# Fixing ScalarE's order in the output projections of a two-layer trunk

## The chip, the cores and the metric

The kernel runs on one core of a Trainium2 chip. The metric is the device time of one execution in microseconds (us); the median over some executions counts. The core has a matrix engine (TensorE, PE in the profile), a vector engine (VectorE, DVE), an engine for activation functions and copies (ScalarE, ACT), GpSimd (POOL, unused here) and SyncE (SP), which issues the DMAs. Each engine works through its own queue in order; semaphores make one wait for another.

## The reference

Two layers of a transformer-like trunk over 3 blocks of 128 tokens (one block of context, two of a sample), 1024 features each. Every layer has a mixer (retention and windowed attention in layer 0, differential attention and Fourier mixing in layer 1), whose concatenated output goes through an output projection, and then a gated FFN with 2816 hidden features. What matters here, for one layer:

```python
out = concat([...], -1) @ w_out                          # output projection, 1024 -> 1024
x = layer_norm(ALPHA * x + g1 * out, ln_g[l, 0], ln_b[l, 0])
u = layer_norm(x) * (1.0 + sc2) + sh2                    # input of the FFN
ffn = (silu(u @ w_gate) * (u @ w_up)) @ w_down
x = layer_norm(ALPHA * x + g2 * ffn, ln_g[l, 1], ln_b[l, 1])
```

All tensors are float32; `sh2`, `sc2`, `g1`, `g2` come from a conditioning vector by `w_mod`.

## The kernel before

A float32 product is made of three passes of a faster matmul type: each operand is split into a rounded part (`r`, a cast on ScalarE) and the rest (`l`, a subtraction on VectorE), and r·r, l·r and r·l are added in PSUM (`in_block`, L372). Weights arrive by DMA into 5 raw buffers and are split by `split` (L172): `S.copy` at L173, `V.tensor_tensor` at L175. A split weight sits in one of 5 pairs of buffers (`wr`, `wl`).

The change is in `w_out_phase` (L435), which runs once in each layer, between the mixer and the FFN. It has these steps, for the blocks b = 0, 1, 2:

- P (`project`): the output projection of a block, in two halves of 512 columns with 24 matmuls each (tiles `wo`), then residual and sums on VectorE (tile `so`), and the first square of the layer norm on ScalarE (L298).
- A and B (`norm`): the rest of the first layer norm (VectorE L366, then a square on ScalarE), and then the second layer norm's scaling into `so` (L313, on ScalarE; for block 2 L311, on VectorE). Each of the two needs a chain of eight small VectorE instructions (L189 to L201, and L309 at the end of the second), an inverse square root.
- F (`to_u`, by way of `make_u` and `make_u_half`): eight row transposes of `so` on TensorE (tiles `puo`), eight scalings by `sc2` and `sh2` (tiles `ufo`, L330, ScalarE; half of block 2's on VectorE, L327), two casts to the rounded part `urf` (L333, ScalarE) and two subtractions to the rest `ulf` (L334, VectorE).
- G and U: load and split the first 256 columns of the gate and the up matrix, in two units each (`r_gh`, `l_gh`, `r_uh`, `l_uh`).
- H (`head`): 24 matmuls of the first gate columns (tile `hg`), a Silu (tile `hsg`, L484, ScalarE), 24 matmuls of the first up columns (tile `hu`) and the product (L487, VectorE); the transposes of this product (tile `ht`) follow in the next head. `hg` and `hu` take turns in two PSUM banks, so that the next head's `hg` needs the bank which the Silu reads.
- X (`hold_splits`): from here on, VectorE's half of each weight split and of each scaling in `mod_steps` has to come after block 2's last `ulf` on VectorE. (`gated`, L169). M is empty in both layers.

`WORDER` (L38) lists the steps for each layer. Its order is the order of priority, not the order in the queues: a planner goes over all instructions with its own model of their durations, and each engine's queue takes the instruction that is ready in that model and stands first in the source; transposes and some matmuls have their priority raised (`boost`). `tc.issue_after(ins)` adds an edge without a wait: the instructions of its block that run on the engine of `ins` are queued behind `ins`. Instructions of the FFN and of `mod_steps` (the conditioning for later, tiles `mraw` and `z`: a DMA, a scaling on ScalarE at L247, additions on VectorE at L250) can move into this phase where the model sees an engine idle.

Of the kernel before, what the change touches and what calls it, by code (L numbers as in the profile page):

```python
# [14 lines left out]
AF = mybir.ActivationFunctionType  # L15
# [4 lines left out]
P = 128  # L20
# [5 lines left out]
NFP = D_FF // 256  # L26
HOLD = 4
RHOLD = (3, 5)
WMODS = ((), ())
TMODS = ()  # L30
SMODS = (((0, 5), (1, 1), (1, 0), (1, 3), (1, 4), (1, 2)), ((1, 5),))
NLNW = 8
# [2 lines left out]
NFILL = 2  # L35
NBUSY = 12
LOADS = (("m", 0, 1), ("kv", 0), ("m", 1, 1), ("q", 0), ("m", 2, 2), ("q", 2), ("m", 4, 2), ("kv", 4), ("q", 4), ("m", 6, 2), ("q", 6))
WORDER = ("P0 P1 G A0 B0 F0 A1 B1 P2 U H0 F1 A2 B2 F2 X H1 M H2", "G P0 P1 A0 B0 A1 B1 U P2 F0 F1 H0 A2 B2 F2 X H1 M H2")  # L38
CORDER = "V0 V1 N0 V2 C N1 N2"
DORDER = "D0 A0 D1 B0 A1 F0 U B1 D2 T A2 F1 B2 F2 K"  # L40
NWR = 5
# [23 lines left out]
def trunk_kernel(ctx: ExitStack, tc: tile.TileContext, a: dict):  # L65
    nc = tc.nc
    mm = nc.tensor.matmul
    V, S, G, SY = nc.vector, nc.scalar, nc.gpsimd, nc.sync
# [47 lines left out]
    def boost(f, *args, **kw):  # L116
        with tc.high_priority(offset=BOOST):
            return f(*args, **kw)  # L118
# [24 lines left out]
    ones = ones_all[:, 0:32]  # L143
# [20 lines left out]
        SY.dma_start(t, src)  # L164
        return t

    gate = [None]

    def gated():  # L169
        return tc.issue_after(gate[0].ins) if gate[0] is not None else nullcontext()  # L170

    def split(t, r, lo):  # L172
        S.copy(r, t)  # L173
        with gated():
            V.tensor_tensor(lo, t, r, ALU.subtract)  # L175
        return r, lo

    def split_unit(src, shape, name, rl=None):
        t = raw_unit(src, shape, f"raw_{name}")
        if rl is None:  # L180
            rl = (perm.tile([P] + shape, F32R, tag="wr", name=f"r_{name}", bufs=NWR),
                  perm.tile([P] + shape, F32R, tag="wl", name=f"l_{name}", bufs=NWR))
        return split(t, rl[0], rl[1])
# [53 lines left out]
    def mod_steps(l, v, out):  # L237
        w = a["w_mod"][l].rearrange("(p k) n -> p k n", k=KC)
        bm = mod_tile(l, v)
        z = [big([P, D], f"z{l}_{v}_{c}") for c in range(2)]  # L240
        for k in range(KC):
            t = big([P, D], f"mraw{l}_{v}_{k}")
            SY.dma_start(t, w[:, k, v * D : (v + 1) * D])
            for c in range(2):
                if k == 0:
                    with gated():
                        S.mul(z[c], t, cs[:, c, k : k + 1])  # L247
                else:
                    with gated():
                        V.scalar_tensor_tensor(z[c], t, cs[:, c, k : k + 1], z[c], ALU.mult, ALU.add)  # L250
            yield k == KC - 1
        ps = bankA(f"mod{l}_{v}")
        for c in range(2):
            for j in range(4):
                mm(ps[32 * j : 32 * j + 32, c * 256 : (c + 1) * 256], ones, z[c][:, j * 256 : (j + 1) * 256],
                   start=True, stop=True)

        if v in (2, 5):
            V.scalar_tensor_tensor(bm, ps[:, 0:256], selc[:, 0:1], bm, ALU.mult, ALU.add)
        else:  # L260
            V.tensor_scalar(bm, ps[:, 0:256], selc[:, 0:1], None, ALU.mult)
        V.scalar_tensor_tensor(bm, ps[:, 256:512], selc[:, 1:2], bm, ALU.mult, ALU.add)
        out.append((bm, ps))
# [31 lines left out]
    def acc_stats(src, junk, sums, name):  # L295
        w = perm.tile([P, 8], F32, tag="lnw", name="lnw" + name, bufs=NLNW)
        V.tensor_scalar(w[:, 0:1], sums[:, 0:1], sums[:, 1:2], -1.0 / D, ALU.add, ALU.mult)
        S.activation(junk, src, AF.Square, bias=w[:, 0:1], accum_out=w[:, 1:2])  # L298
        return w

    def var_rsqrt(w, name):
# [4 lines left out]
    def make_xh(x, xh, w, name, fast=False):  # L306
        rs = var_rsqrt(w, name)
        nmr = w[:, 2:3]
        last = V.tensor_scalar(nmr, w[:, 0:1], rs, None, ALU.mult)  # L309
        if fast:  # L310
            V.tensor_scalar(xh, x, rs, nmr, ALU.mult, ALU.add)  # L311
        else:
            S.activation(xh, x, AF.Identity, bias=nmr, scale=rs)  # L313
        return last

    def make_u_half(b, xh, uf, sh, sc, u, bank, name, hb, fast=False):
        ur, ul = u
        c = cond_of(b)
        cols = slice(b * P, (b + 1) * P)
        pt = bank(f"pu{name}_{hb}")  # L320
        for q in range(4):
            k = hb * 4 + q
            boost(nc.tensor.transpose, pt[:, q * P : (q + 1) * P], xh[:, k * P : (k + 1) * P], ident)
        for q in range(4):
            k = hb * 4 + q
            if fast and q >= 2:
                V.tensor_scalar(uf[:, q, :], pt[:, q * P : (q + 1) * P], sc[:, c, k : k + 1], sh[:, c, k : k + 1],  # L327
                                ALU.mult, ALU.add)
            else:
                S.activation(uf[:, q, :], pt[:, q * P : (q + 1) * P], AF.Identity,  # L330
                             bias=sh[:, c, k : k + 1], scale=sc[:, c, k : k + 1])
        ks = slice(hb * 4, hb * 4 + 4)
        S.copy(ur[:, ks, cols], uf)  # L333
        return V.tensor_tensor(ul[:, ks, cols], uf, ur[:, ks, cols], ALU.subtract)  # L334

    def ln_chain(b, x, s, sums, lnv, name, junk, fast=False, final=False):
# [95 lines left out]
        r, lo = split_unit(w[:, 2 * i : 2 * i + 2, nh * 512 : (nh + 1) * 512], [2, 512], f"wo{l}_{nh}_{i}", rl)  # L432
        return r, lo, 2, 2 * i

    def w_out_phase(l, pre, cat, x, gt, lnv, u2, sh2, sc2, wx, hh, bankTO, mods):  # L435
        bk = Banks(f"pw{l}", W=3, V=1)
        nx = 4 - len(pre)
        units = {0: [wo_unit(l, 0, i) for i in KORDER[l]]}
        units[1] = pre + [wo_unit(l, 1, i, extra_rl(wx, nx, f"{l}{i}")) for i in KORDER[l][len(pre) :]]
        units2, st = {}, {}  # L440

        def head_units(nm, src):
            v = src[l].rearrange("(k p) f -> p k f", p=P)
            units2[nm] = []
            for i in range(2):
                r, lo = split_unit(v[:, 4 * i : 4 * i + 4, 0:256], [4, 256], f"{nm}h{l}_{i}")
                units2[nm].append((r, lo, 4, 4 * i))

        def project(b):
            s = big([P, D], f"so{l}_{b}")  # L450
            sums = small([P, 2], "rsum")
            for nh in range(2):
                ps = bk("V" if (b, nh) == (1, 1) else "W", f"wo{l}_{nh}_{b}")
                in_block(ps, cat, units[nh], b, 512)
                residual(s, x[b], ps, gt, b, nh, sums)
            st[b] = s, ln_chain(b, x[b], s, sums, lnv, f"o{l}_{b}", junk[0], b == 2)
            next(st[b][1])

        last = {}

        def norm(b):
            next(st[b][1])

        def to_u(b):
            tags = iter((None, "WV", "WW")[b] or ())
            bank = bankTO if b == 0 else lambda nm: bk(next(tags), nm)
            last[b] = make_u(b, st[b][0], sh2, sc2, u2, f"o{l}_{b}", bank, b == 2)

        def mod_all():
            for ll, v in mods:  # L470
                mod_now(ll, v, bk("W", f"mw{ll}_{v}"))

        def hold_splits():
            gate[0] = last[2]

        heads = []

        def head(b):
            ps = bankA(f"hg{l}_{b}")
            in_block(ps, u2, units2["g"], b, 256)  # L480
            if heads:
                head_end(*heads.pop())
            sg = mid([P, 256], f"hsg{l}_{b}")
            S.activation(sg, ps[:, 0:256], AF.Silu)  # L484
            ps = bankA(f"hu{l}_{b}")
            in_block(ps, u2, units2["u"], b, 256)
            V.tensor_tensor(sg, ps[:, 0:256], sg, ALU.mult)  # L487
            heads.append((b, sg))

        def head_end(b, sg):  # L490
            pt = bankTO(f"ht{l}_{b}")
            for q in range(NHEAD):
                nc.tensor.transpose(pt[:, q * P : (q + 1) * P], sg[:, q * P : (q + 1) * P], ident)
            cat_split(hh, 0, NHEAD, slice(b * P, (b + 1) * P), pt[:, 0 : NHEAD * P])

        run_order(WORDER[l], {"P": project, "A": norm, "B": norm, "F": to_u, "H": head,
                              "G": lambda: head_units("g", a["w_gate"]), "U": lambda: head_units("u", a["w_up"]),
                              "M": mod_all, "X": hold_splits})
        bk.close()
        return lambda: head_end(*heads.pop())  # L500

# [3 lines left out]
    def ffn_phase(l, u2, x, lnp, hh, wx_es, pto, get_g, lnv, steps, keep, late, tail_units, tail_block, tail_mod, end_heads):  # L505
# [86 lines left out]
        gt = get_g()  # L592
        for fc in range(NH0 + HOLD, NF):
            held[fc] = load_down(fc)
        gate[0] = None
        ss, ch = {}, {}

        def last_down(b):
# [29 lines left out]
        else:  # L628
            for b in range(NB):
                last_down(b)  # L630
                next(ch[b])
                keep(b, x[b])
        gate[0] = None
        accp.close()
        fes.close()

# [720 lines left out]
    for l in range(2):  # L1357
# [31 lines left out]
        u2 = new_u(f"f{l}")  # L1389
        wx, wx_es = opened(f"wx{l}")  # L1390
        hh = tuple(lnp.tile([P, NHEAD, NTOK], F32R, name=f"hh{q}{l}") for q in "rl")
        end_heads = w_out_phase(l, pre, cat, x, gt, lnv, u2, m[l, 3], m[l, 4], wx, hh, bankTO, WMODS[l])
        if wxr_es is not None:
            wxr_es.close()
        cat_es.close()
# [132 lines left out]
```

## Time and profile before

| | us |
|---|---|
| median of 3 runs | 1015.73 (1014.62 to 1015.8) |
| the profiled execution | 1014.2 |
| its span, from the first to the last instruction | 1012.4 |
| TensorE busy in the span | 984.8 |
| VectorE busy | 667.7 |
| ScalarE busy | 436.6 |

Busy times are those of one profiled execution. The span begins with the first instruction and ends with the last; the profiled execution's own time is 1.8 us longer. A matmul's record is longer than its share of the array's time, since matmuls overlap in the pipeline: those of 512 columns are recorded at about 0.39 us and follow one another about every 0.23. In the timelines, the brackets at the end of a row give how long the engine stood idle before it, and what released it.

### The profile page before, as it was taken

The numbers are of one execution on the slowest core, as the hardware profiler recorded it, in microseconds if no ns is written. First come the engines' busy times: TensorE is split into PE (matmuls) and PEld (weight loads), VectorE is DVE, ScalarE is ACT, GpSimd is POOL, SyncE is SP. The second block draws the span as 40 slices with busy tenths as digits, with TensorE's granted clock in tenths as the row PEclk, the third lists the DMA queues.
The fourth block names the chain that finished last, engine by engine and source line by source line (L and its number), as shares of the span: only waits on it lengthen the run. The fifth ranks groups of instructions, "written<-read, shape, count | busy, mean of one in ns | idle before, by whom it ended". The sixth has DMA issues, their size and how long they took to land.

```text
span 1012.4 us, 14717 instructions
## 1 busy us (share of the span) xinstructions
PE 984.8 (97%) x5583; PEld 824.2 (81%) x5583; DVE 667.7 (66%) x1368; ACT 436.6 (43%) x790; POOL 1.2 (0%) x5
## 2 busy tenths in 40 slices
PE   9999999999999999999999999999899999999996
PEld 4775567787899988989887766787799999999985
DVE  5387558588875877968788577558895333335554
ACT  3385533227533343334327555544943333333410
POOL 0000000000000000000000000000000000000000
PEclk9999999999999999999999999999999999999999
DMA  9975446473674877767754333235574544444401
GB/s 304 296 205 188 147 133 205 174 254 111 195 230 137 281 224 249 219 216 227 253 163 153 99 95 94 84 104 225 163 246 153 163 126 126 124 126 124 149 22 42
DMA packets 109704, 172.85 MB, mean 171 GB/s; under 512 B 10177, under 2 KB 78273, under 8 KB 109633
## 3 DMA queue, kind: packets, MB, share of 16 engines
q1 hardware_dynamic: 106960, 170.87, 53.0%
q10 hardware_dynamic: 2672, 1.04, 0.4%
q8 instruction: 44, 0.72, 0.3%
q14 instruction: 28, 0.22, 0.1%
HBM read 167.52 MB, written 4.36 MB: 170 GB/s over the span
## 4 chain that ended last, share of the span: by engine, by line
PE 81%; DVE 6%; ACT 6%; DMA 5%; issue 2%; SPq 0%; ACTq 0%; DVEq 0%
PE dn L544 18%; PE wg L524 15%; PE wu L524 14%; PE cd L378 7%; PE wo L378 4%; PE rvg L378 4%; PE s L378 3%; PE rqk L378 2%; PE mod L118 1%; DMA mraw<-in_w_mod 1%; DMA rawm<-in_w_mod 1%; DMA raw_wd<-in_w_down 1%; PE ms L118 1%; PE hg L378 1%; ACT ufo L330 1%
## 5 line engine op out<-in xcount | busy, mean ns | idle before, releaser
L250 DVE SCALAR_TENSOR_TENSOR z<-mraw,cs,z 128x1024 f32<-128x1024 f32 x98 | 121.5, 1281 | 12.2 <-DMA mraw<-in_w_mod 11.8
L524 PE MATMUL wu<-urf,r_wu 128*128 128x384 f32 x320 | 108.6, 340 | 1.2 <-ACT sg L565 1.2
L524 PE MATMUL wg<-urf,r_wg 128*128 128x384 f32 x320 | 108.2, 340 | 0.4 <-DVE sg L572 0.4
L524 PE MATMUL wu<-ulf,r_wu 128*128 128x384 f32 x320 | 108.3, 338 | 0.0
L524 PE MATMUL wg<-ulf,r_wg 128*128 128x384 f32 x320 | 108.2, 338 | 0.0
L524 PE MATMUL wg<-urf,l_wg 128*128 128x384 f32 x320 | 108.1, 338 | 0.0
L524 PE MATMUL wu<-urf,l_wu 128*128 128x384 f32 x320 | 108.0, 338 | 0.0
L175 DVE TENSOR_TENSOR l_wg<-raw_wg,r_wg 128x1024 fp32r<-128x1024 f32 x40 | 48.8, 1223 | 56.6 <-ACT r_wg L173 56.6
L173 ACT CAST r_wd<-raw_wd 128x1024 fp32r<-128x1024 f32 x36 | 37.8, 1050 | 94.5 <-PE wu L524 44.2
L175 DVE TENSOR_TENSOR l_wd<-raw_wd,r_wd 128x1024 fp32r<-128x1024 f32 x36 | 44.0, 1222 | 47.9 <-ACT r_wd L173 47.9
L173 ACT CAST r_wg<-raw_wg 128x1024 fp32r<-128x1024 f32 x40 | 42.0, 1050 | 74.3 <-PE dn L544 28.5
L175 DVE TENSOR_TENSOR l_wu<-raw_wu,r_wu 128x1024 fp32r<-128x1024 f32 x40 | 48.5, 1223 | 35.0 <-ACT r_wu L173 35.0
L173 ACT CAST r_wu<-raw_wu 128x1024 fp32r<-128x1024 f32 x40 | 42.0, 1050 | 57.6 <-issue 18.9
L544 PE MATMUL dn<-l_wd,hr 128*128 128x512 f32 x168 | 66.6, 396 | 0.0
L544 PE MATMUL dn<-r_wd,hr 128*128 128x512 f32 x168 | 66.5, 396 | 0.0
L544 PE MATMUL dn<-r_wd,hl 128*128 128x512 f32 x168 | 66.5, 396 | 0.0
L524 PEld LDWEIGHTS wu<-urf,r_wu 128*128 128x128 f32 x320 | 60.1, 188 | 3.6 <-ACT sg L565 2.0
L524 PEld LDWEIGHTS wg<-urf,r_wg 128*128 128x128 f32 x320 | 60.1, 188 | 2.6 <-issue 1.2
L524 PEld LDWEIGHTS wu<-ulf,r_wu 128*128 128x128 f32 x320 | 60.1, 188 | 0.5
L524 PEld LDWEIGHTS wg<-ulf,r_wg 128*128 128x128 f32 x320 | 60.1, 188 | 0.4
L524 PEld LDWEIGHTS wu<-urf,l_wu 128*128 128x128 f32 x320 | 60.1, 188 | 0.1
L524 PEld LDWEIGHTS wg<-urf,l_wg 128*128 128x128 f32 x320 | 60.1, 188 | 0.0
(415 smaller groups left out, 2163.9 us busy)
## 6 DMA issues: line engine op xcount, KB each, us to landing
mraw<-in_w_mod SPq DMA_DIRECT2D x56, 512.0 KB
raw_wd<-in_w_down SPq DMA_DIRECT2D x44, 512.0 KB
raw_wg<-in_w_gate SPq DMA_DIRECT2D x40, 512.0 KB
raw_wu<-in_w_up SPq DMA_DIRECT2D x40, 512.0 KB
rawm<-in_w_mod SPq DMA_DIRECT2D x24, 512.0 KB
raw_cd<-in_w_in_cd SPq DMA_DIRECT2D x20, 512.0 KB
ms<-in_w_mod SPq DMA_DIRECT2D x16, 512.0 KB
raw_rqk<-in_w_in_ab SPq DMA_DIRECT2D x16, 256.0 KB
```

The lines of the kernel that those rows point to most:

```text
L118: return f(*args, **kw)
L173: S.copy(r, t)
L175: V.tensor_tensor(lo, t, r, ALU.subtract)
L250: V.scalar_tensor_tensor(z[c], t, cs[:, c, k : k + 1], z[c], ALU.mult, ALU.add)
L330: S.activation(uf[:, q, :], pt[:, q * P : (q + 1) * P], AF.Identity, bias=sh[:, c, k : k + 1], scale=sc[:, c, k : k + 1])
L378: op = mm(ps[:, col : col + width], u[pu][:, k0 + kk, b * P : (b + 1) * P], (r, lo)[pw][:, kk, :], start=(first and i == 0 and pu + pw == ...
L524: mm(ps[j][:, 0:NTOK], un[i][pw][:, k, j * P : (j + 1) * P], u2[pu][:, 4 * i + k, :], start=(i == 0 and k == 0 and pu + pw == 0), stop=(i ...
L544: mm(acc[b, nh], h[fc][ph][:, b * P : (b + 1) * P], wrl[pw][:, nh * 512 : (nh + 1) * 512], start=(fc == 0 and ph + pw == 0), stop=(last an ...
```

## The change

`WORDER` gets new lists, steps G and U are split into single units, step Y (`after_norms`) is new, and step M is gone. ScalarE gets a gate of its own, `gate_s`, beside VectorE's `gate`. `last_s`, `last_split`, `last_t` and `last_p2` remember the last ScalarE instruction of a norm or of F, the last cast of a weight split, the last row transpose and the last matmul of a projection. By them:

- From Y on (after B0 and B1) the casts of weight splits come after block 1's `so` on ScalarE, and so does a Silu of one column, which needs the Silu table.
- F0's ScalarE instructions come after the last cast of U1. The second half of block 2's projection comes after F0's last transpose on TensorE, and the transposes of F1 and F2 after the last matmul of that projection.
- A head's Silu comes after the last ScalarE instruction traced so far: H0's after F1, H1's and H2's after F2.
- From X on, the casts of weight splits and the first scalings in `mod_steps` come after F2's last cast on ScalarE.

```diff
-WORDER = ("P0 P1 G A0 B0 F0 A1 B1 P2 U H0 F1 A2 B2 F2 X H1 M H2", "G P0 P1 A0 B0 A1 B1 U P2 F0 F1 H0 A2 B2 F2 X H1 M H2")
+WORDER = ("P0 P1 G0 A0 B0 A1 B1 Y G1 U0 U1 F0 P2 F1 H0 A2 B2 F2 X H1 H2", "G0 P0 P1 A0 B0 A1 B1 Y G1 U0 U1 F0 P2 F1 H0 A2 B2 F2 X H1 H2")
...
-    gate = [None]
-
-    def gated():
-        return tc.issue_after(gate[0].ins) if gate[0] is not None else nullcontext()
+    gate, gate_s = [None], [None]
+    last_s, last_split, last_t = [None], [None], [None]
+
+    def gated(g=gate):
+        return tc.issue_after(g[0].ins) if g[0] is not None else nullcontext()
 
     def split(t, r, lo):
-        S.copy(r, t)
+        with gated(gate_s):
+            last_split[0] = S.copy(r, t)
         with gated():
             V.tensor_tensor(lo, t, r, ALU.subtract)
...
                 if k == 0:
-                    with gated():
+                    with gated(gate_s):
                         S.mul(z[c], t, cs[:, c, k : k + 1])
...
-        S.activation(junk, src, AF.Square, bias=w[:, 0:1], accum_out=w[:, 1:2])
+        last_s[0] = S.activation(junk, src, AF.Square, bias=w[:, 0:1], accum_out=w[:, 1:2])
...
-            S.activation(xh, x, AF.Identity, bias=nmr, scale=rs)
+            last_s[0] = S.activation(xh, x, AF.Identity, bias=nmr, scale=rs)
...
-            boost(nc.tensor.transpose, pt[:, q * P : (q + 1) * P], xh[:, k * P : (k + 1) * P], ident)
+            last_t[0] = boost(nc.tensor.transpose, pt[:, q * P : (q + 1) * P], xh[:, k * P : (k + 1) * P], ident)
...
-        S.copy(ur[:, ks, cols], uf)
+        last_s[0] = S.copy(ur[:, ks, cols], uf)
...
-                in_block(ps, cat, units[nh], b, 512)
+                with tc.issue_after(last_t[0].ins) if (b, nh) == (2, 1) else nullcontext():
+                    last_p2[0] = in_block(ps, cat, units[nh], b, 512)
...
-            last[b] = make_u(b, st[b][0], sh2, sc2, u2, f"o{l}_{b}", bank, b == 2)
-
-        def mod_all():
-            for ll, v in mods:
-                mod_now(ll, v, bk("W", f"mw{ll}_{v}"))
+            with tc.issue_after((last_split, last_p2, last_p2)[b][0].ins):
+                last[b] = make_u(b, st[b][0], sh2, sc2, u2, f"o{l}_{b}", bank, b == 2)
+
+        def after_norms():
+
+            gate_s[0] = last_s[0]
+            tiny = small([P, 1], "silu")
+            with gated(gate_s):
+                boost(S.activation, tiny, ones[:, 0:1], AF.Silu)
 
         def hold_splits():
             gate[0] = last[2]
+            gate_s[0] = last_s[0]
...
-            S.activation(sg, ps[:, 0:256], AF.Silu)
+            with tc.issue_after(last_s[0].ins):
+                S.activation(sg, ps[:, 0:256], AF.Silu)
...
-        gate[0] = None
+        gate[0] = gate_s[0] = None
```

## Rows read from the trace of the kernel before

**Rows 1.** The profile page, part 1: busy us of each engine, its share and instructions.
```profile
PE 984.8 (97%) x5583; PEld 824.2 (81%) x5583; DVE 667.7 (66%) x1368; ACT 436.6 (43%) x790; POOL 1.2 (0%) x5
```

**Rows 2.** Waits of PE, whole span: us in total, times, longest us.
```profile
PE hg L378 <- DVE ulf L334: 3.1, 6, 1.0
...
PE hg L378 <- ACT urf L333: 1.8, 2, 1.0
...
PE hg L378 <- ACT hsg L484: 1.3, 1, 1.3
...
PE ht L493 <- DVE hsg L487: 0.6, 1, 0.6
```

**Rows 3.** Timeline of ACT, layer 0: start us, us, engine, line, operation, out<-in.
```profile
236.38 1.98 ACT L173 CAST r_uh<-raw_uh 128x1024 fp32r<-128x1024 f32 x2
...
239.31 1.25 ACT L313 ACTIVATE so<-x,lnwbo 128x1024 f32<-128x1024 f32 x1
...
241.60 1.83 ACT L330 ACTIVATE ufo<-puo,modc,modc 128x128 f32<-128x128 f32 x5
243.31 0.63 ACT L333 CAST urf<-ufo 128x512 fp32r<-128x512 f32 x1
...
244.85 1.27 ACT L313 ACTIVATE so<-x,lnwbo 128x1024 f32<-128x1024 f32 x1
...
247.65 2.21 ACT L247 ACTIVATE z<-mraw,cs 128x1024 f32<-128x1024 f32 x2
249.88 1.28 ACT L484 ACT_TABLE_LOAD   x1
...
251.45 1.85 ACT L330 ACTIVATE ufo<-puo,modc,modc 128x128 f32<-128x128 f32 x5
...
254.71 1.19 ACT L298 ACTIVATE so<-x,lnwbo 128x1024 f32<-128x1024 f32 x1
...
256.35 0.41 ACT L392 CAST hhr<-ht 128x256 fp32r<-128x256 f32 x1
...
261.27 0.39 ACT L484 ACTIVATE hsg<-hg 128x256 f32<-128x256 f32 x1
261.55 1.31 ACT L333 CAST urf<-ufo 128x512 fp32r<-128x512 f32 x2
```

**Rows 4.** Timeline of DVE, layer 0.
```profile
235.03 1.22 DVE L175 TENSOR_TENSOR l_gh<-raw_gh,r_gh 128x1024 fp32r<-128x1024 f32 x1
...
242.73 0.15 DVE L189 TENSOR_SCALAR lnwbo<-lnwbo 128x1 f32<-128x1 f32 x1
...
244.00 0.21 DVE L309 TENSOR_SCALAR lnwbo<-lnwbo 128x1 f32<-128x1 f32 x1
...
256.02 0.15 DVE L189 TENSOR_SCALAR lnwbo<-lnwbo 128x1 f32<-128x1 f32 x1 [1.49 <-ACT so L298]
...
258.30 0.81 DVE L311 TENSOR_SCALAR so<-x,lnwbo 128x1024 f32<-128x1024 f32 x1
```

**Rows 5.** Timeline of PE, layer 0, matmuls alone.
```profile
237.38 0.40 PE L378 MATMUL wo<-xrp,catr 128*128 128x512 f32 x1
...
240.61 1.09 PE L118 MATMUL puo<-ident,so 128*128 128x128 f32 x8
...
245.47 0.39 PE L378 MATMUL hg<-r_gh,ulf 128*128 128x256 f32 x1 [0.98 <-DVE ulf L334]
...
251.80 0.28 PE L378 MATMUL hu<-l_uh,urf 128*128 128x256 f32 x1
...
262.95 0.39 PE L378 MATMUL hg<-r_gh,ulf 128*128 128x256 f32 x1 [0.35 <-DVE ulf L334]
```

**Rows 6.** Timeline of ACT, layer 1.
```profile
711.78 1.25 ACT L313 ACTIVATE so<-x,lnwbo 128x1024 f32<-128x1024 f32 x1
```

**Rows 7.** Timeline of PE, layer 1.
```profile
734.11 0.39 PE L378 MATMUL hg<-r_gh,ulf 128*128 128x256 f32 x1 [0.34 <-DVE ulf L334]
```

**Rows 8.** Two stretches: us, busy by engine (instructions), granted PE clock, DMA share, GB/s.
```profile
725.00:730.00 5.00, 3.67 (x31) 3.67 (x32) 2.95 (x12) 4.25 (x7) 0.00 (x0) 1.00 0.66 211
...
1005.00:1012.00 7.00, 0.00 (x0) 0.00 (x0) 4.08 (x15) 1.24 (x2) 0.00 (x0) 0.68 0.20 75
```

More of the change, by code (lines that the diff above doesn't have):

```diff
@@ L28 @@
 RHOLD = (3, 5)
-WMODS = ((), ())
 TMODS = ()
@@ L433, in wo_unit, with w_out_phase @@
         return r, lo, 2, 2 * i
-    def w_out_phase(l, pre, cat, x, gt, lnv, u2, sh2, sc2, wx, hh, bankTO, mods):
+    def w_out_phase(l, pre, cat, x, gt, lnv, u2, sh2, sc2, wx, hh, bankTO):
         bk = Banks(f"pw{l}", W=3, V=1)
@@ L439, in w_out_phase, with head_unit @@
         units[1] = pre + [wo_unit(l, 1, i, extra_rl(wx, nx, f"{l}{i}")) for i in KORDER[l][len(pre) :]]
-        units2, st = {}, {}
-        def head_units(nm, src):
+        units2, st, last_p2 = {}, {}, [None]
+        def head_unit(nm, src, i):
             v = src[l].rearrange("(k p) f -> p k f", p=P)
[L444 to L447, printed above, removed]
+            r, lo = split_unit(v[:, 4 * i : 4 * i + 4, 0:256], [4, 256], f"{nm}h{l}_{i}")
+            units2.setdefault(nm, []).append((r, lo, 4, 4 * i))
         def project(b):
@@ L496, in w_out_phase @@
         run_order(WORDER[l], {"P": project, "A": norm, "B": norm, "F": to_u, "H": head,
-                              "G": lambda: head_units("g", a["w_gate"]), "U": lambda: head_units("u", a["w_up"]),
-                              "M": mod_all, "X": hold_splits})
+                              "G": lambda i: head_unit("g", a["w_gate"], i), "U": lambda i: head_unit("u", a["w_up"], i),
+                              "Y": after_norms, "X": hold_splits})
         bk.close()
@@ L632, in ffn_phase @@
                 keep(b, x[b])
-        gate[0] = None
+        gate[0] = gate_s[0] = None
         accp.close()
@@ L1391, in trunk_kernel @@
         hh = tuple(lnp.tile([P, NHEAD, NTOK], F32R, name=f"hh{q}{l}") for q in "rl")
-        end_heads = w_out_phase(l, pre, cat, x, gt, lnv, u2, m[l, 3], m[l, 4], wx, hh, bankTO, WMODS[l])
+        end_heads = w_out_phase(l, pre, cat, x, gt, lnv, u2, m[l, 3], m[l, 4], wx, hh, bankTO)
         if wxr_es is not None:
```

## The prediction

> **What bounds the kernel now.** I read the page first. TensorE is busy for 97% of the span [rows 1], so a change pays only where TensorE stands still or is made to. Second, the waits of TensorE over the whole span: in the two output-projection phases (layer 0 at about 203 to 270 us, layer 1 at about 676 to 741 us) the head matmuls `hg` and the head transposes `ht` waited 3.1 + 1.8 + 1.3 + 0.6 = 6.8 us in all, for ScalarE's rounding `urf`, VectorE's rest `ulf` and ScalarE's Silu [rows 2]. That is all there is to gain here. Third, ScalarE's and VectorE's timelines of layer 0 [rows 3, 4] against TensorE's [rows 5]: ScalarE runs without a gap from the casts at 236.38 to 256.35, and that queue holds things nobody needs yet: two scalings `z` at 247.65, 2.21 us, and the table load at 249.88, which stands ahead of block 1's scalings. So the order on ScalarE is what these waits hang on.
>
> **The change on ScalarE, layer 0.** Before, the three head casts (`r_gh`'s second, two `r_uh`) ran while ScalarE would have waited for VectorE's chain of block 0: the two `r_uh` at 236.38, and only then `so` (the normalised block 0) at 239.31 [rows 3]. Afterwards step Y puts the Silu table and all three casts behind block 1's normalised `so`, and block 0's scalings (F0) behind the last cast. I follow that queue.
>
> Block 0's `so`: VectorE loses `l_gh` at 235.03 from its queue ahead of it, 1.22 us [rows 4], so it moves from 239.31 to 238.2. Bounds: 237.9 (the square that feeds it ends where the casts began, 236.38, and one VectorE chain takes 1.53 us, from 242.73 to the end of the instruction at 244.00 and its hand-over [rows 4]) and 239.3 (nothing gained).
>
> Block 1's `so`: 238.2 + 1.25 for block 0's `so` + 1.31 for the square (from 254.71 to the first VectorE step at 256.02) + 1.53 for the chain = 242.3 [rows 3, 4]. Before it was 244.85, because two `l_uh` and block 0's scalings stood ahead; bounds 241.9 and 244.85.
>
> Behind it: 1.25 for itself, 1.28 for the table load, at most 0.28 for the one-column Silu (a whole Silu row, 261.27, gives way to the next after that; no row shows one column, lower bound 0; I take the upper), three casts at 0.99 (1.98 for two) = 2.95. F0 begins at 242.3 + 5.8 = 248.1, where it began at 241.60. Its first `urf` is ready 2.34 us later (1.71 from 241.60 to 243.31, and 0.63), at 250.4 [rows 3].
>
> The row shows the load at 1.28 us, starting 0.02 us after `z` has ended [rows 3]. By the Trainium skill (ScalarE: Activation LUTs, What ACT_TABLE_LOAD costs) a switch of tables costs a drain of 1.38 us besides; the rows show no such gap on either side of the load, and by that rule the sum below would be up to 1.4 us more in each layer.
>
> **The change on TensorE, layer 0.** The second half of block 2's projection must now follow block 0's row transposes. The first half ends where the second began, at 237.38; the transposes come 1.30 us after `so` (239.31 to 240.61), now at 239.5 [rows 3, 5]: a new wait of 2.1 us (0.5 + 1.3 = 1.8 to 3.2). Behind it stand the eight transposes (0.8 in the queue), 24 matmuls at 0.231 (14 of them from 237.38 to 240.61) = 5.5, and block 1's transposes, 0.8: TensorE is through at 246.6. Head H0 needs F0's `urf` at 250.4 and 0.7 later its `ulf` (the waits of this kind were 0.5 on average, 1.0 the longest [rows 2]): 3.8 us of standing still, and the stretch of H0 that began at 245.47 begins at 251.1. The first wait costs nothing of its own: H0 hangs on ScalarE anyway.
>
> **What is given back later.** H0 has 5.65 us of matmuls (245.47 to 251.92 without the transposes in it [rows 5]): to 256.75. ScalarE: F0 takes 3.7 us (a block, 251.45 to 256.35 less the square of 1.19 in it [rows 3]) to 251.8, block 2's first square to 253.0, F1 to 256.7, H0's Silu, which must now follow F1, to 257.0. H1's gate matmuls need the bank that this Silu reads: 257.05. H1 with block 2's transposes and H0's (5.65 + 0.8 + 0.15) ends at 263.6. Block 2's second square follows at 257.0, VectorE can start at 258.3, the normalised block is due at 259.8 (258.30 before), and F2's last `urf` ends 4.56 us behind that (258.30 to 262.86 [rows 3, 4]), at 264.4. H1's Silu, which was done in the midst of F2 at 261.27, must now follow it: 264.8, and H2's first matmul waits for its bank. H2 ran from 262.95 on [rows 5], or 262.83 for its first matmul without a break: **+2.0 us**. So most of the 5.6 us comes back, since H1 and H2 no longer meet `z`, the table load or a late cast.
>
> **Layer 1.** The same chain, 472.47 us later (239.31 against 711.78 [rows 3, 6]). There H2 was earlier by that clock: 734.11 [rows 7] is 261.64 on layer 0's scale, since only single `z` scalings stood in its way. 264.8 against 261.5 gives **+3.3 us**.
>
> **Parts that I cost at nothing.** The FFN's first casts and the `z` scalings, held back behind F2's last `urf`: they come while H2 has 5.65 us of matmuls ready, and their VectorE halves were held by the older gate already; if that cover were gone, each late cast would cost its 0.99 us. The weight loads on SP that wait for the raw buffers of the head casts start some 10 us later, still 15 us ahead of their casts; later than that, a load would show as a wait of `r_wd` or `r_wu` for a DMA. Splitting steps G and U, and dropping M (its list is empty), adds no instruction.
>
> **Sum.** +2.0 + 3.3 = +5.3 us on the profiled execution, 1014.2 (span 1012.4 and 1.8 around it): 1019.5. The median of the runs is 1015.73, 1.5 above the profiled one, so I forecast 1021.0. The ends: with block 1's `so` at 241.9 and ScalarE never the later of the two, H2 starts at 263.2, +0.4 and +1.7, 1017.8; with `so` at 244.85 as before, 2.55 more in each layer, 1026.1.
>
> **Rivals.**
> Faster: the relief wins. The casts and the table load fall into ScalarE's waits, F0 is ready when TensorE is done with block 2, and nothing unneeded stands ahead of blocks 1 and 2 any more. All 6.8 us [rows 2] would bring 1008.9; half of it brings 1012.3, which I take. It decides at F0's begin: to lose nothing at H0, F0 must start by 242.4, before block 1's `so` is even normalised; for a gain over both layers it must start some 2.7 us before my 248.1. For it: some 3.2 us of `z` and FFN casts (2.21 and 0.99) really leave layer 0's queue. Against it: the casts used to fill waits of ScalarE that now stay empty (236.4 to 238.2 and 240.7 to 242.3), which is as much. Chance 0.17.
>
> No change: the planner, which still orders VectorE, brings block 1's chain forward and the two shifts cancel, 1015.7. It needs F0 2.7 us earlier, beyond my bound of 0.4, in one layer and less in the other. That the change doesn't act as told belongs here too; but the casts stood ahead of block 0's `so`, so the source's order cannot be what the planner had chosen. Chance 0.11.
>
> Slower still: the clock falls. In the last 7 us of the span TensorE has no work, and the granted clock there is 0.68 on average, where it is 1.00 around the longest wait of these phases [rows 8]; the wait before H0 would be 3.8 us with nothing on TensorE, against 1.3 for the longest here [rows 2]. At the lower level (1.2 GHz) H0's 5.65 us could take up to twice as long in each layer, less 1.2 us by which TensorE is ahead of ScalarE at H2: up to 8.9 us, half of it 1025.5. The Trainium skill (TensorE: Matmul & The Clock Gate, Part 1: The HAM clock gate) has idle stretches return the array to half rate; by that rule this case is near. Chance 0.08.
>
> **How the numbers follow.** Forecast 0.64 (1017.8 to 1024.5 alone), no change 0.11, faster 0.17, clock 0.08. Slower by over 0.2% (2 us, about what a measurement tells from no change) takes the first and last: 0.72; same 0.11; faster 0.17. The range goes from 1013.0, which leaves out most of the faster case, to 1024.5, which leaves out most of the clock's and the far end of mine: about 0.8 is in.
>
> **What would show it.** On ScalarE's timeline after block 1's `so`: table load, one-column Silu, three casts, then F0, near 248 and not 242. On TensorE: a wait of about 2 us ahead of block 0's transposes, and one of 3 to 4 us for `urf` ahead of H0 in each layer; waits for `urf` and `ulf` at H1 and H2 at most as before. `hg` waiting in all 10 us or more against 6.8. I am wrong if F0 starts before 245.3, or if H2 of layer 0 starts before 262.8.

## The result, and the profile after

The changed kernel takes 1025.04 us (median of 4 runs, 1024.73 to 1025.24); the kernel before, run beside it, 1015.76. The ratio is 1.0091, with a 95% interval of 1.0074 to 1.0109: slower by 9.3 us, where 5.3 were forecast. The time lies 0.5 us above the forecast's range.

Part 1 of the page after, and the waits of TensorE over the whole span (us in total, times, longest), to be read against [rows 1] and [rows 2]:

```profile
PE 987.9 (97%) x5583; PEld 828.5 (81%) x5583; DVE 669.2 (65%) x1368; ACT 437.5 (43%) x792; POOL 1.2 (0%) x5
```
```profile
PE puo L117 <- ACT so L315: 7.5, 2, 3.8
PE hg L380 <- ACT hsg L491: 3.7, 2, 1.9
...
PE wg L531 <- DVE sg L579: 1.4, 1, 1.4
...
PE wu L531 <- ACT sg L572: 1.3, 1, 1.3
...
PE puo L117 <- DVE so L313: 0.4, 2, 0.2
```

The waits for `urf` and `ulf` ahead of the heads are gone from this list. In their place stand two long ones for block 0's `so`, one in each layer, and two of 1.9 us for H1's Silu. TensorE also counts 3.1 us more of busy time for the same 5583 matmuls, so some of them ran slower.

ScalarE's timeline of layer 0 after. In this execution the phase began 1.53 us later than in the one before (block 0's first square at 226.59 against 225.06), so 1.53 is to be taken off before a time is compared with [rows 3].

```profile
239.73 1.15 ACT L300 ACTIVATE so<-x,lnwbo 128x1024 f32<-128x1024 f32 x1 [2.07 <-issue]
...
241.53 2.45 ACT L315 ACTIVATE so<-x,lnwbo 128x1024 f32<-128x1024 f32 x2 [0.56 <-DVE lnwbo L311]
244.00 1.28 ACT L117 ACT_TABLE_LOAD   x1
245.29 0.20 ACT L117 ACTIVATE silu<-ones 128x1 f32<-128x1 f32 x1
245.40 1.03 ACT L175 CAST r_gh<-raw_gh 128x1024 fp32r<-128x1024 f32 x1
246.34 2.00 ACT L175 CAST r_uh<-raw_uh 128x1024 fp32r<-128x1024 f32 x2
248.24 1.84 ACT L332 ACTIVATE ufo<-puo,modc,modc 128x128 f32<-128x128 f32 x5
...
259.02 1.15 ACT L300 ACTIVATE so<-x,lnwbo 128x1024 f32<-128x1024 f32 x1 [1.48 <-DVE lnwbo L299]
...
265.25 1.31 ACT L335 CAST urf<-ufo 128x512 fp32r<-128x512 f32 x2 [0.16 <-DVE ufo L329]
266.47 0.38 ACT L491 ACTIVATE hsg<-hg 128x256 f32<-128x256 f32 x1
```

The order is the one that the source asks for. Block 0's and block 1's `so` run back to back (x2): block 0's is late. VectorE's timeline shows why; its chain for block 0 begins at 237.71 and its last step at 241.23, with block 1's norm and block 2's residual between its steps:

```profile
237.71 0.15 DVE L191 TENSOR_SCALAR lnwbo<-lnwbo 128x1 f32<-128x1 f32 x1
237.83 0.75 DVE L368 SCALAR_TENSOR_TENSOR x<-x,lnwao,lnv 128x512 f32<-128x512 f32 x1
...
239.70 0.69 DVE L360 TENSOR_TENSOR so<-wo,g 128x512 f32<-128x512 f32 x1
...
240.42 0.69 DVE L361 SCALAR_TENSOR_TENSOR so<-x,so 128x512 f32<-128x512 f32 x1
...
241.23 0.21 DVE L311 TENSOR_SCALAR lnwbo<-lnwbo 128x1 f32<-128x1 f32 x1
```

In the kernel before, this chain was already mixed with block 1's norm and took 2.7 us, from 236.51 to 239.22 (VectorE's timeline before):

```profile
236.51 0.15 DVE L189 TENSOR_SCALAR lnwbo<-lnwbo 128x1 f32<-128x1 f32 x1
...
239.01 0.21 DVE L309 TENSOR_SCALAR lnwbo<-lnwbo 128x1 f32<-128x1 f32 x1
```

TensorE's timeline of layer 0 (against [rows 5]), and four windows with the granted clock as the first number behind the engines:

```profile
238.67 0.40 PE L380 MATMUL wo<-l_wo,catr 128*128 128x512 f32 x1
242.83 1.67 PE L117 MATMUL puo<-ident,so 128*128 128x128 f32 x8 [3.76 <-ACT so L315]
...
244.72 0.63 PE L380 MATMUL wo<-xrp,catl 128*128 128x512 f32 x1
245.15 0.63 PE L380 MATMUL wo<-xlp,catr 128*128 128x512 f32 x1
...
246.97 0.40 PE L380 MATMUL wo<-xrp,catl 128*128 128x512 f32 x1
247.21 0.40 PE L380 MATMUL wo<-xlp,catr 128*128 128x512 f32 x1
...
251.69 0.37 PE L380 MATMUL hg<-r_gh,urf 128*128 128x256 f32 x1
...
266.90 0.45 PE L380 MATMUL hg<-r_gh,urf 128*128 128x256 f32 x1 [1.85 <-ACT hsg L491]
```
```profile
243.00:247.00 4.00, 4.00 (x16) 3.44 (x16) 0.54 (x1) 3.97 (x5) 0.00 (x0) 0.57 0.01 2
267.00:271.00 4.00, 4.00 (x21) 4.00 (x22) 2.25 (x4) 3.31 (x4) 0.00 (x0) 0.57 0.22 52
720.00:725.00 5.00, 4.10 (x15) 3.63 (x16) 1.11 (x6) 4.97 (x6) 0.00 (x0) 0.66 0.02 3
745.00:749.00 4.00, 4.00 (x33) 4.00 (x34) 3.04 (x4) 4.00 (x5) 0.00 (x0) 1.00 0.15 36
```

TensorE stands still for 3.76 us ahead of block 0's transposes, and then the granted clock is at its lower level, 1.2 GHz: the matmuls of block 2's second half follow one another every 0.43 us (244.72 to 245.15), and every 0.24 again from 246.97 on. H0 starts at 251.69 with no wait at all: what came last for it was not ScalarE but TensorE, through with block 1's transposes only then. The clock falls again at H2 of layer 0: 0.57 and 21 matmuls in the four microseconds from 267, where layer 1's H2 has 1.00 and 33 from 745.

For a sum, each layer's stretch is taken from block 0's first square (L300) to the first Silu of the FFN (L572), both on ScalarE. Before it was 50.34 us in layer 0 and 49.80 in layer 1; after, 54.39 and 53.72: +4.05 and +3.92. The profiled spans differ by 10.5; the other 2.5 are +1.5 ahead of layer 0's stretch, +1.5 between the two and −0.5 behind them. Of these the first is no matter of the change: over all kernels below that start lay between 224.5 and 228.0.

### The profile page after: what moved, and what is told of

The parts are those of the page before. It is cut to its first block, busy times and chain, and to the rows that moved or that the text cites. A ratio compares the mean times of both kernels' runs of the same rounds, so it can differ in the third digit from the quotient of the medians.

```text
span 1022.9 us, 14715 instructions
## 1 busy us (share of the span) xinstructions
PE 987.9 (97%) x5583; PEld 828.5 (81%) x5583; DVE 669.2 (65%) x1368; ACT 437.5 (43%) x792; POOL 1.2 (0%) x5
## 4 chain that ended last, share of the span: by engine, by line
PE 61%; DVE 6%; ACT 3%; DMA 2%; issue 1%; SPq 0%; ACTq 0%; DVEq 0%
PE dn L551 18%; PE wg L531 15%; PE wu L531 15%; PE cd L380 7%; PE wo L380 2%; DMA mraw<-in_w_mod 2%; DVE z L252 1%; DMA raw_wd<-in_w_down 1%; PE hg L380 1%; ACT dp L1241 1%; PE mod L257 1%; PE dpv L117 1%; PE hu L380 1%; PE ds L117 0%; DVE dnm L1236 0%
```

## The experiments

Twelve kernels were timed, in four groups, each beside the kernel before on the same chip (medians there 1016.04, 1015.95, 1015.04 and 1015.75). The table has, for each: the median and the ratio to before with its interval; what each layer's stretch gained or lost in the profiled execution; and the time that the lowered clock took from TensorE in each, summed over windows of 1 us as 1 less the granted clock. Where the clock fell before a wait had ended, the part within the wait (up to 0.9 us of a stretch) cost nothing.

| kernel | us | ratio to before | stretch, layer 0 / 1 | clock's loss, layer 0 / 1 |
|---|---|---|---|---|
| the change | 1025.04 | 1.0091 (1.0074 to 1.0109) | +4.05 / +3.92 | 3.4 / 1.7 |
| block 2's second half free | 1019.94 | 1.0029 (1.0014 to 1.0044) | +1.35 / +2.68 | 3.4 / 1.7 |
| casts free | 1022.41 | 1.0057 (1.0034 to 1.0079) | +1.76 / +2.96 | 1.7 / 1.7 |
| both free | 1015.44 | 0.9994 (0.9978 to 1.0010) | −1.14 / +0.19 | 0 / 0 |
| head's Silu free | 1022.15 | 1.0054 (1.0035 to 1.0074) | +2.15 / +4.66 | 1.7 / 3.4 |
| all three free | 1012.79 | 0.9963 (0.9952 to 0.9975) | −2.21 / −0.93 | 0 / 0 |
| hold free | 1020.74 | 1.0044 (1.0026 to 1.0061) | +1.55 / +3.68 | 0 / 3.4 |
| filled wait | 1019.58 | 1.0039 (1.0024 to 1.0053) | +1.05 / +2.39 | 0 / 0 |
| block 0's chain first | 1022.74 | 1.0077 (1.0063 to 1.0090) | +2.78 / +4.09 | 1.7 / 1.7 |
| three and hold free | 1012.21 | 0.9969 (0.9956 to 0.9981) | −2.23 / −0.90 | 0 / 0 |
| three free, no early load | 1011.51 | 0.9963 (0.9951 to 0.9976) | −2.22 / −0.87 | 0 / 0 |
| order alone | 1014.50 | 0.9991 (0.9977 to 1.0004) | −0.01 / +0.02 | 1.7 / 0 |
| hold alone | 1012.98 | 0.9970 (0.9959 to 0.9982) | −1.74 / −0.88 | 0 / 0 |

**Block 2's second half free.** One edge of the change undone:

```diff
-                with tc.issue_after(last_t[0].ins) if (b, nh) == (2, 1) else nullcontext():
+                with nullcontext():
```


> The second half of block 2's projection no longer follows block 0's row transposes; all else as changed. Theory A: head H0 hangs on two things that end nearly together in the changed kernel (ScalarE's queue with the table load and three casts, and TensorE's queue behind the transposes, slowed by the clock), so that freeing TensorE alone moves the wait to H0, where ScalarE's urf is awaited for some 4 us, and the clock falls there instead: 1020.5 to 1023.5. Rival B: the forced order on TensorE, with the fall of the clock behind its 3.8 us wait, is the whole cost: 1016 to 1018.5. Rival C: ScalarE's queue alone is the cost, TensorE's order is free: 1024 to 1026.

**Casts free.** The three casts and block 0's scalings freed:

```diff
-            with tc.issue_after((last_split, last_p2, last_p2)[b][0].ins):
+            with tc.issue_after(last_p2[0].ins) if b else nullcontext():
...
-            gate_s[0] = last_s[0]
             tiny = small([P, 1], "silu")
-            with gated(gate_s):
+            with tc.issue_after(last_s[0].ins):
```


> The three head casts may run wherever ScalarE is free, and block 0's scalings no longer follow them; the early table load, TensorE's order and the held FFN casts stay. Theory A: block 0's scalings start near 242 again, but the transposes are still awaited for 2 to 4 us and the clock still falls, and now this sets H0: 1018 to 1022. Rival B (TensorE's order is the whole cost): 1023 to 1026. Rival C (ScalarE's queue alone): 1014 to 1017.

**Both free.** The two edits together.

> Both at once: TensorE's order and the casts freed. Theory A: the two did not add in the changed kernel, so that only both together bring back what each layer lost: 1011 to 1016, no fall of the clock in either layer, and with the Silu edges left the H2 wait for hsg stays at 1 us or more. Rivals B and C: 1016 to 1018.5, no better than the one of the two that each names.

**Head's Silu free.** It no longer has to follow F1 or F2:

```diff
-            with tc.issue_after(last_s[0].ins):
+            with nullcontext():
                 S.activation(sg, ps[:, 0:256], AF.Silu)
```


> A head's Silu no longer has to follow F1 or F2 on ScalarE; all else as changed. Theory: H1's Silu behind F2's last cast holds the bank that H2 needs, 1.85 us in each layer, and lets the clock fall in H2 of layer 0 (1.5 us): without it 0.8 to 1.5 us come back in each layer and the fall of layer 0 may go, 1021 to 1023.5. Rival: block 2's own scalings end when H2 starts anyway, so that the wait only changes its name to urf: 1024.5 to 1025.5.

With either edge gone a cost is left (1.0029, 1.0057), with both gone none that can be told from zero (0.9994): this is theory A's pattern, and the theories that put the whole cost on one edge fall. Theory A's own ranges for the single edges were missed by half a microsecond (1019.94 against 1020.5 to 1023.5, 1022.41 against 1018 to 1022). Its claim that the two don't add isn't shown either: over the kernel's time the single gains, 0.62% and 0.34%, make up the 0.97% of both, and only in layer 1's stretch is their sum (2.2 us) well below what both gain (3.7). With block 2's second half free, TensorE no longer waits for block 0's `so`; it goes on to the end of block 2 and waits there. TensorE's timeline and two windows of this kernel:

```profile
249.61 0.58 PE L380 MATMUL hg<-r_gh,urf 128*128 128x256 f32 x1 [4.00 <-ACT urf L335]
```
```profile
248.00:249.00 1.00, 0.00 (x0) 0.00 (x0) 1.00 (x2) 1.00 (x5) 0.00 (x0) 0.50 0.84 291
...
249.00:255.00 6.00, 5.35 (x24) 5.05 (x25) 5.77 (x20) 6.00 (x16) 0.00 (x0) 0.53 0.65 207
```

That is the forecast's wait of 3.8 us ahead of H0, at 4.0, and the clock falls with it, here already before its end: 0.50 from 248 to 249, with nothing on TensorE. Freeing the head's Silu takes the waits of 1.9 us at H2 with it; 0.9 for `urf` and 0.3 for `ulf` come in their place.

**Filled wait.** The change whole, and four matmuls into a spare bank, on which nothing depends, where TensorE stood still (each is recorded as two):

```diff
+                if (b, nh) == (2, 0):
+                    with tc.issue_after(last_p2[0].ins):
+                        keep_busy(4, bankA(f"fill{l}"), ident, gt[:, 0, 0:512])
                 residual(s, x[b], ps, gt, b, nh, sums)
```


> The change whole, with four matmuls into a spare PSUM bank between the halves of block 2's projection, where TensorE stood still for 3.8 us ahead of block 0's transposes: nothing that is computed depends on them, so only TensorE's idle time goes. Theory A with the clock (the granted clock of 0.5 behind that wait doubles the pitch of the matmuls up to 246.7 and so makes H0 late): the clock stays at 1.00 behind the transposes, block 2's residual and H0 come 1.5 to 2 us earlier, and the time falls by 1 to 3 us, to 1022 to 1024. Rival E (the clock costs nothing, since H0 and H2 hang on ScalarE's queue alone): the time stays at 1025, H0 only waits longer for urf, by what TensorE gains.

TensorE's timeline of layer 0 and the window behind it:

```profile
238.58 3.60 PE L128 MATMUL fill<-g,ident 128*128 128x512 f32 x8
...
242.50 1.09 PE L117 MATMUL puo<-ident,so 128*128 128x128 f32 x8 [0.33 <-ACT so L315]
...
265.08 0.39 PE L380 MATMUL hg<-r_gh,urf 128*128 128x256 f32 x1 [0.30 <-ACT hsg L494]
```
```profile
243.00:247.00 4.00, 4.00 (x22) 3.37 (x21) 0.86 (x1) 3.97 (x6) 0.00 (x0) 1.00 0.01 2
```

Block 0's transposes come exactly as late as in the changed kernel, 16.24 us after the first square (242.50 − 226.26 and 242.83 − 226.59), and F0 too, 21.65 us after it; only TensorE's stillness is gone. The clock stays at 1.00 in all of both stretches, the matmuls pass at full rate (22 in the window, not 16), and of the 9.3 us 3.6 are left. More work on TensorE made the kernel some 5.5 us faster (1025.04 against 1019.58; the kernel before measured 1015.76 and 1015.95 beside them), and the two intervals do not meet. Rival E falls, and theory A had the gain too small, at 1 to 3 us. The profiled executions are no exception in this: the mean granted clock of an execution was 0.990 to 0.993 in all four of the changed kernel, and 0.997 or 0.998 in eleven of the twelve of this one (0.995 in the other). The 5.5 us are the clock's share, with one reserve: the planner put block 2's first square ahead of F1's scalings here and among them in the changed kernel, and this kernel doesn't part that from the clock.

**Block 0's chain first.** The change whole, and one edge more, by which block 1's norm waits on VectorE until block 0's chain is through:

```diff
...
-            last = V.scalar_tensor_tensor(x[:, h], x[:, h], rs, lnv[:, 1, h], ALU.mult, ALU.add, accum_out=out[:, i : i + 1])
+            with tc.issue_after(c0[0].ins) if c0[0] is not None else nullcontext():
+                last = V.scalar_tensor_tensor(x[:, h], x[:, h], rs, lnv[:, 1, h], ALU.mult, ALU.add, accum_out=out[:, i : i + 1])
...
         def norm(b):
-            next(st[b][1])
+            d = next(st[b][1])
+            nnorm[0] += 1
+            c0[0] = d if nnorm[0] == 2 else None
```


> The change whole, with one edge more: block 1's two normalising passes on VectorE (the first layer norm, 0.75 us each) come after block 0's second chain, which the planner had mixed with them. Theory A (the wait ahead of block 0's transposes is 3.8 us and not the forecast's 2.1 because that chain takes 3.7 us instead of 1.5, and the long wait is what lets the granted clock fall): block 0's so comes 1.5 to 2.2 us earlier, the wait is 1.6 to 2.3 us, the clock stays at 1.00 behind it, block 1's so comes up to 1.3 us later, a wait of 1 to 3 us for urf appears ahead of H0, and the time is 1018 to 1022. Rival F (the clock falls in these stretches whatever the length of the wait, or H0's begin alone counts): clock 0.5 behind the shorter wait too, or the time stays at 1024 to 1026, since ScalarE's queue behind block 1's so only moves later.

TensorE's timeline of layer 0, and the windows behind its two waits:

```profile
238.97 1.09 PE L117 MATMUL puo<-ident,so 128*128 128x128 f32 x8 [1.51 <-ACT so L315]
...
250.45 0.39 PE L381 MATMUL hg<-r_gh,urf 128*128 128x256 f32 x1 [4.00 <-ACT urf L335]
```
```profile
239.00:244.00 5.00, 5.00 (x26) 4.29 (x27) 2.57 (x13) 2.69 (x4) 0.00 (x0) 1.00 0.01 3
250.00:255.00 5.00, 4.22 (x21) 4.02 (x22) 4.76 (x16) 5.00 (x13) 0.00 (x0) 0.66 0.71 232
```

This is the forecast's course as it was written: a short wait ahead of block 0's transposes with the clock at 1.00 behind it, then one of 4.0 us for `urf` ahead of H0. The clock falls there instead, and the time is 1022.74, still 0.8% above before and 0.7 us above what theory A expected, which had the wait ahead of H0 at 1 to 3 us. Its interval overlaps that of the changed kernel: the late chain decided where TensorE stands still, and little that can be told of how much it costs.

**Hold free.**

```diff
             gate[0] = last[2]
-            gate_s[0] = last_s[0]
+            gate_s[0] = None
```


> The change whole, but ScalarE's gate is lifted at X: the FFN's first casts and the z scalings may run before F2's last rounding. Rival D in its second half (the held casts and scalings are what made the stretch from the first FFN Silu of layer 0 to layer 1's first square 422.9 us where it was 421.3): that stretch is back at 421.3 or below and the time is 1 to 2 us under the changed kernel's, 1023. Theory A: the waits ahead of block 0's transposes and ahead of H2 stay, 3.8 and 1.9 us in each layer, and the time stays within 1 us of the changed kernel's, 1025.

The part between the two stretches was 421.65 us, as rival D has it (421.34 before, 422.86 after). But other kernels with the hold lie from 419.8 to 423.5 there, and the one without it and with the three edges free at 422.9, so whether the hold makes FFN 0 lose 1.5 us stays open. The time, 1020.74, lies below what either theory names (1023 and 1025), and the profiled execution (1022.23) shows something that neither has: the same wait in both layers, and the clock fell with one of them alone.

```profile
244.24 1.09 PE L117 MATMUL puo<-ident,so 128*128 128x128 f32 x8 [3.76 <-ACT so L315]
...
267.33 0.39 PE L380 MATMUL hg<-r_gh,urf 128*128 128x256 f32 x1 [0.30 <-ACT hsg L491]
...
718.59 1.97 PE L117 MATMUL puo<-ident,so 128*128 128x128 f32 x8 [3.75 <-ACT so L315]
```
```profile
244.00:249.00 5.00, 4.76 (x25) 4.10 (x26) 1.17 (x2) 4.97 (x7) 0.00 (x0) 1.00 0.01 2
718.00:724.00 6.00, 5.41 (x18) 4.64 (x19) 2.14 (x4) 5.97 (x8) 0.00 (x0) 0.53 0.01 3
```

So this is a second measure of the clock, without matmuls added. In layer 0, where it stayed up, H2 begins 39.33 us after block 0's first square (267.33 − 228.00), against 38.82 in the filled wait and 40.31 in the changed kernel, and the stretch loses 1.55 us, near the filled wait's 1.05 and far from 4.05. Whether lifting the hold has a part in the clock's staying up is not shown.

**All three free.** Casts and F0, block 2's second half, and the head's Silu; the new lists of steps, F1's and F2's edge, the early table load and the hold stay.

> Of the change only the early table load and the casts and scalings held back from X on are left; casts, F0, block 2's second half and the head's Silu are free of the new edges. Theory A (the two orders on F0 and on TensorE are the cost, the Silu behind F2's rounding adds 1.8 us at H2): 1012 to 1015, level with the kernel before or up to 0.3% faster, waits of hg for ScalarE's Silu gone or under 0.5 us, and those for urf and ulf 2 to 5 us in all. Rival D (the early table load and the hold cost time themselves): 1018 or more, with a wait ahead of H0 behind the table load, or casts of the FFN that come late for wg.

Faster than both kernels, 1012.79 against 1015.95, by 0.37% (0.25 to 0.48). The cost of the three edges is thus nearer to 1.3% than to the change's 0.91%: what is kept here gains beside them. The four experiments that remain ask what gains these 3 us. Its waits of TensorE:

```profile
PE hg L380 <- DVE ulf L336: 1.9, 6, 0.3
...
PE hg L380 <- ACT urf L335: 1.6, 2, 0.8
```

In all 3.5 us, against the 6.8 of [rows 2].

**Three and hold free** adds the edit of "hold free":

> The version with the early table load and the hold alone, which measured 1012.8, without the hold on ScalarE: one FFN cast and two z scalings move back into layer 0's stretch between the blocks. Theory G (the hold is what gains on the kernel before): 1014.5 to 1016, level with before, waits ahead of H1 and H2 for urf, ulf or hsg up by 1 to 2 us. Rival H (the early table load gains): 1012 to 1013.5, no change from 1012.8.

**Three free, no early load** keeps the hold and makes `after_norms` empty:

```diff
-            gate_s[0] = last_s[0]
-            tiny = small([P, 1], "silu")
-            with gated(gate_s):
-                boost(S.activation, tiny, ones[:, 0:1], AF.Silu)
+            pass
```


> The version with the early table load and the hold alone, which measured 1012.8, without the early table load: the load stands ahead of H0's Silu again. Theory G (the hold gains): 1012 to 1013.5, no change. Rival H (the table load, 1.28 us, in front of block 0's last scalings instead of H0's Silu gains): 1014.5 to 1016, with H0's Silu and F1's second urf 1.3 us later and a wait ahead of H1.

Each of the two can be left out: both kernels keep the gain, so G and H fall as they were put here. Two more kernels took single parts.

**Order alone**: the lists of steps stay; every edge, the early load and the hold are gone.

> Of the change the lists of steps alone (the second half of block 2's projection, F0 and F1 ahead of H0 in priority): no edge, no early table load, no hold. Theory J (what gains 3 us on the kernel before is that block 1's scalings come before H0's Silu and the table load, and the scalings z come later): 1011.5 to 1013, the table load behind block 1's scalings. Theory G (it is the hold, or either of hold and table load can do it for the other): 1014.5 to 1016.

**Hold alone**: the hold stays; every edge and the early load are gone, and the steps have the order of before.

```diff
-WORDER = ("P0 P1 G0 A0 B0 A1 B1 Y G1 U0 U1 F0 P2 F1 H0 A2 B2 F2 X H1 H2", "G0 P0 P1 A0 B0 A1 B1 Y G1 U0 U1 F0 P2 F1 H0 A2 B2 F2 X H1 H2")
+WORDER = ("P0 P1 G0 G1 A0 B0 F0 A1 B1 P2 U0 U1 H0 F1 A2 B2 F2 X H1 H2", "G0 G1 P0 P1 A0 B0 A1 B1 U0 U1 P2 F0 F1 H0 A2 B2 F2 X H1 H2")
```


> The steps in the order of before (H0 ahead of F1), with the hold on ScalarE's casts and z scalings alone: no edge and no early table load. Theory J: little, 1014 to 1016, since the table load still stands ahead of block 1's scalings. Theory G: 1011.5 to 1013, since the two z scalings, 2.2 us, and one FFN cast leave layer 0's queue; layer 1, which had only single z scalings, gains less.

The hold alone brings 0.30% (0.18 to 0.41), the order alone nothing that can be told from zero (its interval holds 1). J falls; G holds in its second form, that either of hold and load can do it for the other. The hold on ScalarE is worth nearly the whole gain by itself. That the early load gains as much where there is no hold, with the order and F1's and F2's edge beside it, is shown for these together; which of the three does it was not tried. In "order alone" the table load stands ahead of H0's Silu, H1 waits 1.88 us for that Silu, and the clock falls behind this wait in layer 0 (1.7 us), so in the profiled execution the clock may have taken back what the order itself gains; no run parts the two.

## Why the prediction was wrong in size

- **The direction held, and the delay of the heads.** The new orders on F0 and on TensorE make the heads late, and most of it is given back by H2. With the clock held up (filled wait) H0 waits for ScalarE's `urf`, as the forecast has it, and layer 1 loses more than layer 0: 1.05 and 2.39 us, where the forecast has 2.0 and 3.3, each 0.9 to 1.0 too many. Of the signs named beforehand, F0 behind the load and the casts came; the wait of 3 to 4 us for `urf` ahead of H0, and `hg` waiting 10 us or more, did not (none, and 3.7): TensorE's long waits stood ahead of block 0's transposes, 7.5 us in the two layers.
- **ScalarE's queue was costed too dear.** Less 1.53, block 1's `so` (the second of the pair at 241.53) began at about 241.2, not 242.3, and F0 began at 246.7, not 248.1. The one-column Silu, costed at 0.28, delayed the next instruction by 0.11 (245.29 to 245.40), and the square of block 1 ran ahead of block 0's `so`. The table load took 1.28 us and the Silu began 0.01 us behind it. The Trainium skill (ScalarE: Activation LUTs, What ACT_TABLE_LOAD costs) adds a drain of 1.38 us to a switch; this trace shows none on either side, as in [rows 3].
- **The wait ahead of block 0's transposes was sized at 2.1 us (1.8 to 3.2) and was 3.76.** The forecast took 1.53 us for VectorE's chain, from block 1's chain in the trace before; block 0's took 3.7 from its start to the end of L311's row, since the planner put other work between its steps, and had taken 2.7 in the kernel before. This moved the long wait from H0, where the forecast had it, to block 0's transposes. It is a miss, but "block 0's chain first" has the short wait and the long one at H0, and is 0.8% slower than before all the same.
- **The step that failed is the clock's fall, which the sum puts at nothing.** By the sum the wait ahead of block 0's transposes "costs nothing of its own", since H0 hangs on ScalarE anyway, and it leaves the fall to a rival with a chance of 0.08, although its own sum had TensorE stand still for 3.8 us where 1.3 was the longest in these phases. In the changed kernel the clock fell behind this wait in both layers, the slower matmuls of block 2 made TensorE the last that H0 hangs on, and with the wait filled some 5.5 us of the 9.3 were gone.
- **What the falls cost.** Of the twelve waits of 3.05 to 4.00 us that the profiles of these phases hold (two in each of six kernels), all but one had a fall. It took 1.7 us or 3.4 of TensorE's time, less than the "twice as long" of the text for one head, but it came in both layers and a third time at H2, and it delayed block 2's residual (its second square had to wait 1.48 us for VectorE at 259.02, and 0.18 in the filled wait) and so F2 and H2. The Trainium skill's rule (TensorE: Matmul & The Clock Gate, Part 1: The HAM clock gate), that idle stretches bring the array back to half rate, agrees with the 0.50 that the granted clock shows for 1 us or more in each of these falls; the one wait of 3.76 us without a fall is not explained by any run here.
- **That the rival's 1025.5 lies so near 1025.04 is luck in part.** It took half of its greatest cost, for a fall behind a wait ahead of H0, on top of a sum that was 1.9 us too dear over both stretches; the falls came elsewhere. The sum's own far end, 1026.1, lies above the measured time too, but by a late `so` of block 1 (244.85), which came at 241.2.
- **By the profiled execution:** H2 of layer 0 began at 265.4 on the old scale (266.90 − 1.53) against a forecast of 264.8, and layer 1's is 0.6 late as well; the fall at H2 adds 1.5 in layer 0. FFN 0 adds 1.5, where `wu` and `wg` wait 1.3 and 1.4 near its end (before, 0.8 and 0.4); the text had the held casts at nothing, and whether it is they stays open. With this one's late start (+1.5) and −0.5 at the end that makes 5.2 beside the forecast's 5.3, and the span's 10.5.
- **The faster rival's relief exists**, but not through the order. What it named for itself, `z` and FFN casts leaving layer 0's queue, gains 0.3% when it is done alone.

## What to carry to other kernels

Where your own sum makes the busiest engine stand still for longer than any wait in the trace before, the fall of the clock belongs into the main case, and with it what the slower matmuls delay behind them. When two orders lead to the same step, freeing one may only move the wait to the other: undo them one by one and together before blaming one. When a bundle of edges is slower, one of them may still be good: here holding back work that nobody needs yet was worth 0.3% by itself, and the rest of the bundle hid it.

## What the runs showed of the hardware

- The same wait of TensorE, 3.76 and 3.75 us in one execution, was followed by a granted clock of 1.00 in one layer and came with one of 0.53 in the other. Of eight waits of 1.84 to 1.88 us, two were followed by a fall (layer 0 of the changed kernel, and of "order alone"). The fall is not a fixed consequence of the wait's length alone.
- Matmuls whose result nobody reads, 3.6 us of them in each layer, held the granted clock at 1.00 in both stretches and took some 5.5 us off the time.
